# Three-layer transformer in one launch: single scoring in the third mixer's window attention, and a wider in-flight limit in the stick-breaking layer

## The chip, the cores and the metric

The kernel runs on one core of a Trainium2 chip. The metric is the device time of one launch in microseconds (us), the median of several runs. Engines are named as in the profile: PE is the matrix engine (PEld its weight loads), DVE the vector engine, ACT the scalar engine, POOL the GpSimd engine, SP the engine that issues the weight loads by DMA.

## The reference, cut to what matters

256 tokens of width 1024 pass three layers, each a mixer and a convolutional feed-forward net (FFN), in fp32. The mixers differ:

- Layer 1, stick-breaking attention, 16 heads of width 64. For the causal part of a head's scores z, `a = exp(log_sigmoid(z) + suffix)`, where `suffix` is the sum of `log_sigmoid(-z)` over the later keys; the output is `a @ v`.
- Layer 2, a sparse attention that picks keys with an indexer (8 index heads of width 64, 16 attention heads of width 128).
- Layer 3, half window attention, half a gated recurrence. The window attention has 8 query heads of width 64 over 2 key heads:

```python
scores = where(mask, q @ k.T * 64**-0.5, -inf)          # causal window of 128
m = maximum(scores.max(-1), sink)
e = exp(scores - m)
p = e / (e.sum(-1) + exp(sink - m))
out = p @ v
```

Its output is normalised and joined with the recurrence's; one output product follows. The scale, shift and gate vectors of each layer come from a long matrix-vector product of the condition with `ada_w`.

## The kernel before, in words

All activations are kept transposed (features on partitions, 256 tokens along the row). Weights stream from HBM in blocks of 1 MB (`raw`), and each half block of 128x1024 is split into a high and a low part, `wh` on ACT (L409) and `wl` on DVE (L421); a product is three matmuls (`three`, L302: high x high, high x low, low x high). One `unit` (L579) makes 256 output columns from two half blocks, 48 matmuls. Each half block is one *turn*: `next` (L435) counts a tick and releases what earlier turns put off (`after`, `turnover`), the matmuls follow, and `post` (L459) emits a share of the condition's matrix-vector product (`ada_op`, L544: one 512 KB load issued on POOL, L525, and one pass over it on DVE, L532, three buffers) and then takes `rate` steps of the background work (`advance`, L476).

The background work of a mixer is a generator, `heads_in_flight` (L485). A step of it may multiply a pair of finished heads with the values (`product`), do the second stage of one head (`middle`, called `suffix` in layer 1, `flip` in layer 3), and start new heads (`scores`). `a` counts heads started, `c` heads past the second stage; new ones start while `a - c` is below a limit (L491). Its argument `pair` says how many heads one call of `scores` takes, `lag` how many turns lie between a head's scores and its second stage. When a mixer's projections end, `output` (L1103) first lets no head start until none is open (`hold`), then sets `out`, takes the four PSUM banks tagged `acc` for the output product and runs its eight `down` steps between the remaining heads, which now score into the two banks tagged `mm`.

A head keeps its bank from its scores to the end of its second stage. There are four `acc` banks (L310).

- In layer 1 (`stick`, L1003), `scores` (L1034) takes two heads: their four fp32 matmuls have 64 rows each, one head on the upper half of the array's rows, one on the lower, in alternation and `chained` (L316: kept in that order). The softplus of a head runs on ACT (L1051 to L1053, two buffers `e`), DVE (L1057, into `s`, four buffers) and POOL (mask, L1031); `suffix` (L1061) sums with three matmuls, an exponential on ACT and a mask on POOL; `product` (L1070) follows.
- In layer 3 (`mixed`, L1343), `scores` (L1451) also takes two heads in a chain of four 64-row matmuls, adds the mask to each with one more matmul (L1461), and `softmax` (L1464) puts off maximum and exponential by one turn, the division by two. `flip` (L1491) transposes a head's three 128x128 blocks into its own bank and copies them out on ACT (L1129, which frees the bank), `product` (L1494) multiplies a pair with the values, and `window` (L1508) normalises. Then comes `recurrence` (L1598), in the same list of background work: one first step (`acc` banks, L1600), then eight levels, each with decays (`level_decay`, L1554) and scores (`level_scores`, L1577). The first output step needs `window`, the next three need the recurrence.
- In layer 2, `scores` has always taken one head a call.

The Tile framework sets the final order: what the program emits earlier has the higher priority, and a planner with its own model of times lays out each engine's queue, which the engine then works through in order. So a step of the generator sets a priority and not a time.

Of the kernel before, what the change touches and what calls it, by code (L numbers as in the profile page):

```python
# [270 lines left out]
class Prog:  # L271
# [213 lines left out]
    def heads_in_flight(self, n, st, ready, scores, middle, product, lag=2, pair=1):  # L485

        st.update(hold=False, out=False, done=0, open=0, ready=0, split=0)
        a = c = 0
        ticks = {}
        while st["done"] < n:  # L490
            can = a < n and not st["hold"] and ready(a) and a - c < (3 - pair if st["out"] else 4 - pair)  # L491
            did = False
            if st["done"] + 1 < c and (st["done"] % 4 or not st["split"]):
                product(st["done"])
                st["done"] += 2
                did = True
            if c < a and (a - c >= 2 or not can) and self.tick - ticks[c] >= lag and c - st["done"] < WP:
                middle(c)
                c += 1
                did = True  # L500
            if can:
                scores(a)
                for a in range(a, a + pair):
                    ticks[a] = self.tick
                a += 1
                did = True
            st["open"] = a - c
            yield did
# [834 lines left out]
    def mixed(self):  # L1343
        nc, I = self.nc, self.I
        blocks = ((0, slice(0, 128)), (1, slice(128, 384)))
        with ExitStack() as outer:
# [4 lines left out]
            band_r = sk.tile([128, 384], F32R, name="band")  # L1351
# [39 lines left out]
            ka = sk.tile([128, T], F32, name="ka")  # L1391
            va = sk.tile([128, 2, 128], F32, name="va")
            st, part = {}, []
            sp = pool("hgx", 2)
            qa = sp.tile([128, 4, T], F32, name="ro")
# [35 lines left out]
            for half in range(2):  # L1431
                h, l = self.next()
# [10 lines left out]
            def keys():  # L1443
                nc.scalar.activation(ka, bkv[:, 0:T], AF.Identity, bias=self.v("bka"))
                nc.vector.tensor_tensor(va, bkv[:, 256:512].rearrange("p (t c) -> p t c", t=2),
                                        rows[:, None, 512:640].to_broadcast([128, 2, 128]), op=ALU.add)
                self.bg.extend([self.heads_in_flight(8, st, lambda h: True, scores, flip, product, 2, 2), window()])

            Z, E, P, PO = {}, {}, {}, {}

            def scores(h0):  # L1451
                for h in (h0, h0 + 1):
                    Z[h] = self.bank("acc")
                chain = []
                for t, j in ((1, 1), (1, 0), (0, 1), (0, 0)):
                    r = slice(j * 64, j * 64 + 64)
                    chain.append(self.mmul(Z[h0 + j][:, t * 128:128 + t * 256], qa[r, h0 // 2, t * 128:t * 128 + 128],
                                           ka[r, 0:128 + t * 128], start=t == 1))
                self.chained(chain)
                for h in (h0, h0 + 1):  # L1460
                    self.mmul(Z[h][:, 0:384], self.ident_r, band_r, stop=True)  # L1461
                    softmax(h)

            def softmax(h):  # L1464
                i, kv = divmod(h, 2)
                z = Z[h]
                sink = self.v("sink", i + 4 * kv, 1)
                m = sp.tile([128, 4, 2], F32, name="wm", bufs=3)
                e = E[h] = sp.tile([128, 384], F32, name="we", bufs=3)

                def soft():
                    for t, c in blocks:
                        nc.vector.tensor_reduce(m[:, 0, t:t + 1], z[:, c], axis=AX.X, op=ALU.max)
                    nc.vector.tensor_scalar(m[:, 1], m[:, 0], sink, -1.0, op0=ALU.max, op1=ALU.mult)
                    for t, c in blocks:
                        self.act(e[:, c], z[:, c], AF.Exp, bias=m[:, 1, t:t + 1],
                                             accum_out=m[:, 2, t:t + 1])
                    self.act(m[:, 3], m[:, 1], AF.Exp, bias=sink)

                def divide():  # L1480
                    nc.vector.tensor_tensor(m[:, 2], m[:, 2], m[:, 3], op=ALU.add)
                    nc.vector.reciprocal(m[:, 2], m[:, 2])
                    for t, c in blocks:
                        if DM:
                            nc.scalar.activation(e[:, c], e[:, c], AF.Copy, scale=m[:, 2, t:t + 1])
                        else:
                            nc.vector.tensor_scalar(e[:, c], e[:, c], m[:, 2, t:t + 1], None, op0=ALU.mult)
                self.after(1, soft)
                self.after(2, divide)
# [18 lines left out]
            def window():  # L1508
                o = ao
                cs = self.bank("po")  # L1510
                sq, other = [self.squares(o[:, i:i + 2]) for i in (0, 2)]
                nc.vector.tensor_tensor(sq, sq, other, op=ALU.add)
                yield True
                for j in range(2):
                    self.sums(cs[:, 0:2], sq[:, j], j == 0, j == 1)
                rr = self.rsqrt(cs[:, 0:2], 2, 512)
                if FW:
                    self.fence = self.newton[1]
                yield True
                self.spread(cs[:, 256:512], rr, start=False)  # L1520
                for i in range(4):
                    last = nc.vector.scalar_tensor_tensor(o[:, i], o[:, i], self.v("ag", i, 1), cs[:, 256:512], op0=ALU.mult,
                                                   op1=ALU.mult)
                if FW > 1:
                    self.fence = last.ins
                if WS:
                    for i in range(0, 4, WS):
                        self.split_act(oh[:, i:i + WS], ol[:, i:i + WS], o[:, i:i + WS])
                else:
                    self.split_act(oh[:, 0:4], ol[:, 0:4], o)  # L1530
                part.append(0)

            self.after(1, keys)

            def turn():
# [199 lines left out]
```

## Time and profile before

| | us |
|---|---|
| runs of the kernel before | 1038.05, 1036.2, 1028.79; median 1036.2 |
| the profiled execution | 1033.1, of it 1031.4 in its span |
| PE busy | 998.2 (97% of the span) |
| DVE, ACT, POOL busy | 833.5, 636.4, 98.9 |

The span begins with layer 1's norm; its heads lie at 65 to 150 us, its FFN at 160 to 350, layer 2 at 350 to 480 and its FFN to 675, layer 3's mixer at 675 to 830, its FFN to the end. A busy PE is not a PE at its peak: the three-matmul stream places 8.41 matmuls in a us (841 in the 100 us from 200 to 300), and where fewer are placed the difference is waiting or slower forms.

### The profile page before, as it was taken

To read this page: it belongs to the slowest core of one execution; us is meant where nothing else is said; L and a number is where in the kernel's file an instruction comes from. 1 tells how busy PE (TensorE), PEld (TensorE's weight loads), DVE (VectorE), ACT (ScalarE), POOL (GpSimd) and SP (SyncE) were. 2 spreads that over 40 slices of the span, in tenths; PEclk is the share of its full clock that TensorE was granted. 3 is DMA by queue.
4 is the path that set the end of the run, shared out by engine and by line. 5 is a ranking of instruction groups with operands and counts; after the bars stand their busy time and mean duration, and the time that the engine had idled before them with its cause. 6 is when DMAs were issued, how large, how long until landed. Compare 5 with 4: busy or idle time off the path is not lost.

```text
span 1031.4 us, 19958 instructions
## 1 busy us (share of the span) xinstructions
PE 998.2 (97%) x7984; PEld 964.1 (93%) x7984; DVE 833.5 (81%) x1550; ACT 636.4 (62%) x1095; POOL 98.9 (10%) x180
## 2 busy tenths in 40 slices
PE   7999989999999999998999999999999999999996
PEld 5998878999999989988999999999899999999996
DVE  6956768999999889987998889897994588566664
ACT  6575647855555684886965555588854378445543
POOL 0015530011111010110000101100120000000000
PEclk9999989999999999999999999999986999999998
DMA  9969764578888476642767777745880336566531
GB/s 362 405 239 336 243 241 159 209 276 300 290 295 289 142 275 216 241 169 83 268 225 268 283 268 284 277 150 210 306 312 21 124 127 226 200 210 220 211 137 42
DMA packets 45647, 235.66 MB, mean 228 GB/s; under 512 B 5361, under 2 KB 5889, under 8 KB 27889
## 3 DMA queue, kind: packets, MB, share of 16 engines
q1 hardware_dynamic: 25922, 164.21, 44.1%
q0 software_dynamic: 19344, 69.78, 19.3%
q8 instruction: 62, 1.02, 0.4%
q10 hardware_dynamic: 288, 0.39, 0.1%
q14 instruction: 31, 0.25, 0.1%
HBM read 233.29 MB, written 1.07 MB: 227 GB/s over the span
## 4 chain that ended last, share of the span: by engine, by line
PE 81%; issue 8%; DVE 5%; DMA 3%; ACT 2%; POOL 1%; DVEq 0%; SPq 0%; POOLq 0%; ACTq 0%
PE acc L300 32%; PE mm L300 29%; PE po L300 10%; PE small L300 10%; DMA adaw<-ada 2%; DVE x L691 1%; DVE xl L687 1%; POOL adaw L525 1%; DVE wl L421 1%; DVE adaw L532 1%; ACT wh L409 0%; DMA x<-xT 0%; DVE sq L714 0%; PE acc L1126 0%; ACT e L330 0%
## 5 line engine op out<-in xcount | busy, mean ns | idle before, releaser
L409 ACT ACTIVATE wh<-raw 128x1024 fp32r<-128x1024 f32 x290 | 304.7, 1057 | 224.8 <-PE acc L300 87.1
L421 DVE TENSOR_TENSOR wl<-raw,wh 128x1024 fp32r<-128x1024 f32 x290 | 353.0, 1223 | 96.1 <-PE acc L300 27.8
L300 PE MATMUL mm<-xh,wh 128*128 128x256 f32 (+1 forms) x872 | 244.5, 285 | 2.1 <-ACT wh L409 2.1
L300 PE MATMUL mm<-xl,wh 128*128 128x256 f32 (+1 forms) x872 | 245.4, 283 | 0.7 <-DVE xl L687 0.7
L300 PE MATMUL mm<-xh,wl 128*128 128x256 f32 (+1 forms) x872 | 244.3, 282 | 0.0
L532 DVE SCALAR_TENSOR_TENSOR adaw<-adaw,cond 128x1024 f32<-128x1024 f32 x144 | 175.2, 1221 | 10.7 <-DMA adaw<-ada 10.4
L300 PEld LDWEIGHTS mm<-xh,wh 128*128 128x128 f32 x872 | 163.5, 189 | 4.9 <-ACT wh L409 2.7
L300 PEld LDWEIGHTS mm<-xl,wh 128*128 128x128 f32 x872 | 164.6, 189 | 2.3 <-DVE xl L687 1.1
L300 PEld LDWEIGHTS mm<-xh,wl 128*128 128x128 f32 x872 | 164.0, 188 | 0.5 <-issue 0.3
L300 PE MATMUL acc<-gh,wl 128*128 128x256 f32 x528 | 149.0, 283 | 0.0
L300 PE MATMUL acc<-gh,wh 128*128 128x256 f32 x528 | 148.1, 282 | 0.0
L300 PE MATMUL acc<-gl,wh 128*128 128x256 f32 x528 | 147.9, 281 | 0.0
L525 POOL DMA_DIRECT2D adaw<-ada x125 | 66.6, 533 | 738.6 <-DVE adaw L532 624.9
L300 PEld LDWEIGHTS acc<-gl,wh 128*128 128x128 f32 x528 | 100.3, 190 | 0.2 <-DVE gl L337 0.2
L300 PEld LDWEIGHTS acc<-gh,wh 128*128 128x128 f32 x528 | 98.8, 188 | 0.0
L300 PEld LDWEIGHTS acc<-gh,wl 128*128 128x128 f32 x528 | 98.8, 187 | 0.0
L300 PE MATMUL small<-xh,wh 128*128 128x256 f32 x240 | 67.6, 282 | 0.0
L300 PE MATMUL small<-xh,wl 128*128 128x256 f32 x240 | 67.5, 281 | 0.0
L300 PE MATMUL small<-xl,wh 128*128 128x256 f32 x240 | 67.3, 281 | 0.0
L300 PE MATMUL acc<-oh,wh 128*128 128x256 f32 x192 | 53.1, 297 | 2.0 <-ACT oh L336 1.5
L300 PE MATMUL acc<-xh,wl 128*128 128x258 f32 (+1 forms) x192 | 52.4, 284 | 2.1 <-DVE wl L421 2.0
L300 PE MATMUL acc<-ol,wh 128*128 128x256 f32 x192 | 53.7, 286 | 0.4 <-DVE ol L337 0.4
(310 smaller groups left out, 2073.9 us busy)
## 6 DMA issues: line engine op xcount, KB each, us to landing
raw<-ffn SPq DMA_DIRECT2D x99, 1024.0 KB, 5.0
adaw<-ada POOLq DMA_DIRECT2D x125, 512.0 KB, 5.2
raw<-dsa SPq DMA_DIRECT2D x15, 1024.0 KB, 6.4
raw<-hg SPq DMA_DIRECT2D x15, 1024.0 KB, 5.9
adaw<-ada SPq DMA_DIRECT2D x19, 512.0 KB, 10.2
raw<-sb SPq DMA_DIRECT2D x16, 512.0 KB, 10.2
raw<-sb SPq DMA_DIRECT2D x8, 1024.0 KB, 8.5
bias<-scr POOLq DMA_DIRECT2D x8, 256.0 KB, 8.3
```

What stands on the lines that cost most here:

```text
L300: return self.nc.tensor.matmul(o, a, b, start=start, stop=stop, skip_group_check=True).ins
L409: inst = nc.scalar.activation(h[:, :k * n], self.raws[b][:, c0:c0 + k * n], AF.Copy).ins
L421: inst = nc.vector.tensor_tensor(l[:, :k * n], self.raws[b][:, c0:c0 + k * n], h[:, :k * n], op=ALU.subtract).ins
L525: self.nc.gpsimd.dma_start(raw, self.I[f"ada{L}"][b])
L532: return self.nc.vector.scalar_tensor_tensor(w, w, 1.0, self.cond[n // 24], op0=ALU.mult, op1=ALU.mult, accum_out=self.M[n // 12][:, n % 1 ...
L687: return lambda: nc.vector.scalar_tensor_tensor(self.xl[:, m, 0:T], self.x[:, m], a, self.xh[:, m, 0:T], op0=ALU.mult, op1=ALU.subtract)
L691: self.lastx = nc.vector.scalar_tensor_tensor(self.x[:, m], o, self.gate(L, h, m), self.x[:, m], op0=ALU.mult, op1=ALU.add).ins
```

## The change

The limit of heads in flight becomes 3 before `out`, for every caller: for a caller with pairs (layer 1) it was 2, so that a pair now starts while up to two heads are open; for callers with single heads it was 3 already. During `out` the limit stays `3 - pair`. Layer 3 now calls `heads_in_flight` with its defaults (lag 2, pair 1), and its `scores` takes one head, without a chain. The chain in `product` stays.

```diff
@@ heads_in_flight
-            can = a < n and not st["hold"] and ready(a) and a - c < (3 - pair if st["out"] else 4 - pair)
+            can = a < n and not st["hold"] and ready(a) and a - c < ((3 - pair) if st["out"] else 3)
@@ mixed
-                self.bg.extend([self.heads_in_flight(8, st, lambda h: True, scores, flip, product, 2, 2), window()])
+                self.bg.extend([self.heads_in_flight(8, st, lambda h: True, scores, flip, product), window()])
 
-            def scores(h0):
-                for h in (h0, h0 + 1):
-                    Z[h] = self.bank("acc")
-                chain = []
-                for t, j in ((1, 1), (1, 0), (0, 1), (0, 0)):
-                    r = slice(j * 64, j * 64 + 64)
-                    chain.append(self.mmul(Z[h0 + j][:, t * 128:128 + t * 256], qa[r, h0 // 2, t * 128:t * 128 + 128],
-                                           ka[r, 0:128 + t * 128], start=t == 1))
-                self.chained(chain)
-                for h in (h0, h0 + 1):
-                    self.mmul(Z[h][:, 0:384], self.ident_r, band_r, stop=True)
-                    softmax(h)
-
-            def softmax(h):
+            def scores(h):
                 i, kv = divmod(h, 2)
-                z = Z[h]
+                r = slice(kv * 64, kv * 64 + 64)
+                z = Z[h] = self.bank("acc")
+                self.mmul(z[:, 0:128], qa[r, i, 0:128], ka[r, 0:128], start=True)
+                self.mmul(z[:, 128:384], qa[r, i, 128:256], ka[r, :])
+                self.mmul(z[:, 0:384], self.ident_r, band_r, stop=True)
                 sink = self.v("sink", i + 4 * kv, 1)
...
```

## Rows read from the trace of the kernel before

**Rows 1.** The page, part 1: busy time of each engine, share of the span, instructions.
```profile
PE 998.2 (97%) x7984; PEld 964.1 (93%) x7984; DVE 833.5 (81%) x1550; ACT 636.4 (62%) x1095; POOL 98.9 (10%) x180
```

**Rows 2.** Busy time by stage; columns: stretch, length, engines (x instructions), granted clock, DMA.
```profile
65.00:98.00 33.00, 33.00 (x255) 29.84 (x255) 21.57 (x30) 22.61 (x40) 16.15 (x25) 1.00 0.76 276
98.00:108.40 10.40, 8.39 (x63) 6.31 (x62) 6.76 (x12) 8.27 (x20) 3.24 (x7) 1.00 0.81 283
108.40:150.00 41.60, 36.68 (x261) 31.94 (x261) 31.03 (x58) 18.88 (x38) 21.40 (x35) 0.92 0.73 244
200.00:300.00 100.00, 100.00 (x841) 100.00 (x841) 91.64 (x143) 54.84 (x72) 10.61 (x20) 1.00 0.80 282
704.00:759.00 55.00, 53.76 (x440) 50.37 (x439) 48.98 (x105) 44.37 (x102) 9.03 (x17) 1.00 0.77 285
759.00:806.00 47.00, 44.44 (x257) 42.82 (x255) 27.38 (x63) 20.00 (x51) 2.65 (x5) 0.67 0.27 90
```

**Rows 3.** Timeline of PE at a visit to one, four and two heads: start, length, what.
```profile
387.33 0.28 PE L300 MATMUL mm<-xh,wl 128*128 128x256 f32 x1
387.54 0.92 PE L300 MATMUL acc<-ki,qi 64*128 64x128 f32 x4
388.39 0.39 PE L300 MATMUL mm<-xh,wh 128*128 128x256 f32 x1
...
378.64 1.68 PE L300 MATMUL acc<-ki,qi 64*128 64x128 f32 x16
380.26 0.38 PE L300 MATMUL mm<-xh,wh 128*128 128x256 f32 x1
...
707.11 0.92 PE L300 MATMUL acc<-ka,ro 64*128 64x256 f32 x8
707.96 0.62 PE L300 MATMUL acc<-band,ident_r 128*128 128x384 f32 x2
708.42 0.28 PE L300 MATMUL mm<-xh,wh 128*128 128x256 f32 x1
```

**Rows 4.** Timeline of PE, then ACT: the last pair of heads of layer 3.
```profile
732.67 0.70 PE L300 MATMUL acc<-ka,ro 64*128 64x256 f32 x2 [0.76 <-ACT pT L1129]
...
737.73 0.92 PE L300 MATMUL acc<-ka,ro 64*128 64x256 f32 x6
...
734.42 0.49 ACT L1129 ACTIVATE pT<-acc 128x384 f32<-128x384 f32 x1 [0.64 <-PE acc L1126]
```

**Rows 5.** Instructions of the tile qk: duration min/median/max, first and last start.
```profile
L300 PE MATMUL acc<-qk x40: 269/374/481, 65.1 to 103.3; 64*128 64x256 f32 x20, 64*128 64x128 f32 x20
...
L300 PE MATMUL mm<-qk x24: 269/374/480, 97.8 to 136.6; 64*128 64x256 f32 x12, 64*128 64x128 f32 x12
```

**Rows 6.** Timeline of PE in layer 1: scores, and suffix sums of two pairs.
```profile
65.14 1.58 PE L300 MATMUL acc<-qk 64*128 64x256 f32 x16
...
105.86 0.70 PE L300 MATMUL acc<-s,nu 128*128 128x256 f32 x2 [1.50 <-POOL s L1031]
...
112.60 0.60 PE L300 MATMUL acc<-s,nu 128*128 128x256 f32 x2
...
122.67 0.70 PE L300 MATMUL mm<-qk 64*128 64x256 f32 x2
...
135.93 0.92 PE L300 MATMUL mm<-qk 64*128 64x256 f32 x8
```

**Rows 7.** Timeline of all engines at the end of layer 1's heads.
```profile
141.15 1.23 DVE L532 SCALAR_TENSOR_TENSOR adaw<-adaw,cond 128x1024 f32<-128x1024 f32 x1 [0.29 <-DMA adaw<-ada]
...
142.30 1.02 DVE L1057 SCALAR_TENSOR_TENSOR s<-mm,e 128x384 f32<-128x384 f32 x2
...
148.59 0.87 PE L300 MATMUL po<-a,V 128*64 128x256 f32 x8 [1.12 <-POOL a L1031]
...
149.94 0.74 PE L300 MATMUL acc<-oh,wh 128*128 128x256 f32 x4 [0.48 <-ACT oh L336]
```

**Rows 8.** The chain that ended last, 98 to 151 us: start, length, what.
```profile
136.60 4.52 DMA adaw<-ada
```

## The prediction

> **What bounds the kernel now.** I read the page first, then the busy time by stage, then the timelines of the two stretches that the change touches, and last the chain that ends each of them. PE is busy 97% of the span [rows 1], so the question is at what rate it works. In the FFN it places 841 matmuls in 100 us, 8.41 a us, at a granted clock of 1.00 [rows 2]; nothing is to be had there. Two stretches fall behind. In layer 1 from 108.4 to 150 us, where the last heads run between the output's weights, there are 261 in 41.6 us, 6.3 a us; at the FFN's rate they would take 31.0 us. In layer 3 the projections go on until 759 us at 8.0 a us, and then 47 us follow with 257 matmuls, 5.5 a us, at a mean granted clock of 0.67: the tail of the recurrence. The reader should see there that DVE and ACT are only 58% and 43% busy: engines wait for one another.
>
> What ends layer 1's stretch is not the heads alone. The chain [rows 8] passes through a load of `adaw` of 4.52 us; the DVE pass over it runs at 141.15, and heads 14 and 15 have their softplus step at 142.30, right behind it in the same queue; their product follows at 148.59 and the last output step at 149.94 [rows 7].
>
> **Part 1, the limit in layer 1.** I stepped through the generator by hand, two steps a turn, with its own rules. Before, pairs are emitted in turns 0, 1, 3, 4 and 6, so ten heads start before `out` and six after. The trace has it so: 40 matmuls of `qk` into `acc` and 24 into `mm`, four records a head [rows 5]. With the new limit pairs come in turns 0, 0, 2, 3, 4 and 6: twelve heads before `out`, four after, and the last product comes in turn 14 instead of 15. No instruction is added or removed; only priorities move.
>
> What is it worth? Heads in `mm` go one pair at a time: the scores of heads 12 and 13 begin at 122.67, those of 14 and 15 at 135.93 [rows 6], so a pair costs 13.3 us there, and one such pair goes. But the pass at 141.15 needs its load, whichever head is in flight, and the pass ends at 142.3; if the heads were done by then, the last output step could start at 142.3 instead of 149.94, 7.6 us earlier [rows 7]. That is the upper end unless the loads come earlier too. The other side: `hold` now has two more heads to finish before all four `acc` banks go to the output. Two successive pairs there lie 112.60 - 105.86 = 6.7 us apart [rows 6], so the output's weights could start 6.7 us later, with nothing but heads to fill PE, in a stretch where it now places 63 matmuls in 10.4 us [rows 2]. Below both ends stands the fact that at 65.14 sixteen matmuls run together, four heads in the kernel of before [rows 6]: the planner had already filled all four banks, and a higher priority can't make a fifth. So the ends are 7.6 us won and 6.7 us lost. I take 4 us won, about half of the upper end: later pairs do move up a turn, masks and softplus steps with them, and the load that caps it has a row of its own.
>
> **Part 2, single scoring in layer 3.** The pair's chain lays two heads of 64 rows beside each other. Eight records of two heads take 707.96 - 707.11 = 0.85 us, and a single head of the same shape in layer 2, alone, takes 388.39 - 387.54 = 0.85 us [rows 3]. But of the four pairs only two ran whole. The last one (and likewise the third) was broken: its first matmul, 0.70 us, ran at 732.67 as soon as one bank was free, the other six records at 737.73 [rows 4]. So the scores take now 2 x 0.85 + 2 x (0.70 + 0.85) = 4.8 us. After the change: all eight alone, 8 x 0.85 = 6.8 us; but four single heads of layer 2, which no chain orders, took 380.26 - 378.64 = 1.62 us, 0.40 a head [rows 3], because the planner laid them side by side. By the order of emission heads 2 and 3, and 6 and 7, still come in the same turn, 4 x 0.40 + 4 x 0.85 = 5.0 us. I take 5.9, between the two: 1.1 us lost (ends: 1.6 won with all eight in company, 2.0 lost). The mask matmuls: two take 0.46 us behind a pair [rows 3]; one alone costs at least half and at most all of that, so eight cost between nothing and 1.8 us more; I take 0.4, nearer the half, since the form is the same. Entering such a visit costs 387.54 - 387.33 = 0.21 us instead of the 0.12 between two matmuls of the stream [rows 3]; eight visits instead of six add 0.2 us. Together 1.7 us lost on PE, in a stretch that has no slack for it (8.0 of 8.41 a us).
>
> The Trainium skill (TensorEngine Tiling, Theoretical Speedup) gives up to twice the speed for a contraction of 64 rows or less, which speaks against taking pairs apart. This trace agrees where a pair runs whole, 0.85 us for two heads as for one. By the page alone the loss would be 8 x 0.85 - 4 x 0.85 = 3.4 us instead of 1.1, and the whole forecast 2.3 us later.
>
> **Part 3, what the single heads let go earlier.** Now head 6 and head 7 wait for two banks at once. The second was freed at 734.42 + 0.49 = 734.9, the six records came at 737.73, and the first bank lay with a lone matmul from 732.67 [rows 4]; so their softmax could begin 2.8 to 5.1 us earlier. In the generator the last product comes in turn 8 instead of 9, and the recurrence, next in the list, a turn sooner. A turn is 55 us / 14 half blocks = 3.9 us here [rows 2]. What moves out of the tail is work that PE still has to do among the weights: 3.9 us of the tail is 21 matmuls, 2.5 us at 8.41 a us, so 1.4 us are won. Ends: nothing (if the planner had the recurrence's first step where its banks come free anyway) and 5.1 us. I take 1.4. DVE, ACT and POOL have the same instructions as before; in layer 2 the limit is 3 and 2 as before.
>
> **The sum.** 4.0 won in layer 1, 1.7 lost and 1.4 won in layer 3: 3.7 us less. The profiled execution took 1033.1 us (1031.4 in its span), which becomes 1029.4. The median of the runs is 1036.2, 3.1 us above the profiled one, and on that footing the forecast is 1032.5 us.
>
> **Rivals.**
> - *Nothing moves.* The four banks were full before, so priorities change little; layer 1 gives 0, layer 3 0.3 lost, up to 2. For it: 65.14 in [rows 6]. Against it: the broken pairs and the waits for two banks [rows 4] are real. 1036 to 1038 us.
> - *A whole pair goes.* With two heads fewer in `mm`, fewer masks stand on POOL before the loads that it issues, the loads come earlier and the 7.6 us no longer cap the gain. Layer 1 wins 7.6 to 13.3, layer 3 5.1 - 1.7 = 3.4: 1025.2 down to 1019.5 us. For it: the pair's 13.3 us [rows 6]. Against it: the load in the chain [rows 8].
> - *The drain costs more than it saves* (the slower side). Its place is the end of layer 1's projections, its price the 6.7 us by which four banks come free later, while the last pass of `adaw` and what hangs on it shift with the output's turns; with eight lone heads, dear masks and two more visits in layer 3 (2.0 + 1.8 + 0.2 = 4.0), 1036.2 + 10.7 = 1046.9 us. It decides from the point at which the suffix sums of heads 10 and 11 lie more than 7.6 us behind the 112.60 of heads 8 and 9 now: then the pair that is saved later no longer pays.
>
> **How the numbers follow.** Forecast 0.43, nothing moves 0.25, a whole pair 0.18, the drain 0.14. A measurement of this kernel tells about 1% from no change, here 10.4 us: faster means below 1025.8, slower above 1046.6. Faster has most of the second rival (0.15) and a little of the forecast's own spread (0.05): 0.20. Slower has a bit over half of the drain's chance, since milder drains end under the line: 0.09. The rest, 0.71, is the same. The range runs from 1022, inside the second rival, to 1043, inside the drain's; that leaves out about a tenth on each side. The likeliest case alone is 1028 to 1036.
>
> **What would show it.** Right: 48 records of `qk` into `acc` and 16 into `mm`; the last output step of layer 1 at 142 to 148 instead of 149.94; `ka` matmuls in visits of four records, 5.0 to 6.8 us in all; last projection of layer 3 a little after 759, and the tail behind it 1 to 5 us shorter than 47. Wrong: layer 1's output starting after 115 and ending after 150; a pass of `adaw` that still ends the chain with the heads long done (then the cap was all); or a time that moves in an FFN or in layer 2, where nothing was changed.

## The result, and the profile after

The kernel after takes 1024.71 us (median of 20 runs, 1018.71 to 1033.44) against 1031.8 us (20 runs, 1028.45 to 1038.05) for the kernel before: ratio 0.9927, 95% interval 0.9909 to 0.9945. That is 0.73%, 7.5 us (the medians themselves lie 7.1 us apart), about twice the forecast 3.7 us and inside the range. Medians, ratios and mean clocks below are of fast runs; seven of the later runs, 1036.52 us to 5383.13 us long, were in a slow state. The profiled execution took 1025.47 us, 1023.7 of it in its span.

The stages that the change touches, as busy time by stage (columns as in [rows 2]):

```profile
108.40:150.00 41.60, 39.29 (x301) 34.93 (x302) 34.63 (x66) 22.00 (x46) 20.43 (x34) 1.00 0.75 259
704.00:756.00 52.00, 51.97 (x402) 46.74 (x401) 44.92 (x98) 41.77 (x96) 8.46 (x16) 1.00 0.73 262
756.00:796.60 40.60, 37.62 (x274) 35.80 (x272) 29.09 (x68) 22.20 (x55) 3.17 (x6) 0.87 0.38 132
```

Against [rows 2] the end of layer 1's heads places 301 matmuls instead of 261 in the same 41.6 us, at a granted clock of 1.00 instead of 0.92. Layer 3's projections end at 756.0, and the tail behind them is 40.6 us instead of 47.0, at 0.87 instead of 0.67. PE is busy 97% of the span, as before; the reader sees again that this share tells nothing of the rate.

The instructions of the tile `qk`, the counterpart of [rows 5]:

```profile
L300 PE MATMUL acc<-qk x48: 269/374/481, 65.3 to 110.1; 64*128 64x256 f32 x24, 64*128 64x128 f32 x24
...
L300 PE MATMUL mm<-qk x16: 269/374/480, 101.3 to 132.9; 64*128 64x256 f32 x8, 64*128 64x128 f32 x8
```

Twelve heads score into `acc` and four into `mm`; the last one starts at 132.9 instead of 136.6. Then the output's matmuls of layer 1 (tile `oh`), first of the kernel before, then of the kernel after; the last two times of a row are the first and the last start:

```profile
L300 PE MATMUL acc<-oh,wh x64: 277/282/387, 108.4 to 154.4; 128*128 128x256 f32 x64
```

```profile
L300 PE MATMUL acc<-oh,wh x64: 278/281/388, 112.2 to 149.3; 128*128 128x256 f32 x64
```

The output begins 3.8 us later and ends 5.1 us earlier. The chain that ended last there, of the kernel after (start, length, what), the counterpart of [rows 7, 8]:

```profile
139.94 2.30 DVE adaw L532 x4
...
142.27 0.25 DVE mod L558
...
142.53 0.52 POOL adaw L525
...
143.09 0.43 POOL a L1031
...
143.56 0.90 PE po L300 x8
...
144.92 0.99 PE acc L300 x6
```

The last output step runs at 144.92 instead of 149.94. The chain still passes two `adaw` passes, and behind them the mask of the last head on POOL, which stands in POOL's queue after the issue of a load. Whether these passes set the end is not to be read from a chain alone; an experiment below asks it. PE's own timeline of the kernel after already raises a doubt, for PE waited only 0.23 us for that mask:

```profile
143.56 0.87 PE L300 MATMUL po<-a,V 128*64 128x256 f32 x8 [0.23 <-POOL a L1031]
```

Layer 3's single heads on PE, the counterpart of [rows 3]:

```profile
704.56 0.92 PE L300 MATMUL acc<-ka,ro 64*128 64x128 f32 x4
705.41 0.44 PE L300 MATMUL acc<-band,ident_r 128*128 128x384 f32 x1
705.78 0.92 PE L300 MATMUL acc<-ka,ro 64*128 64x128 f32 x4
...
730.88 0.44 PE L300 MATMUL acc<-band,ident_r 128*128 128x384 f32 x1
731.16 0.28 PE L300 MATMUL mm<-wh,xl 128*128 128x256 f32 x1
...
732.99 0.44 PE L300 MATMUL acc<-band,ident_r 128*128 128x384 f32 x1
733.45 0.87 PE L300 MATMUL po<-pT,va 128*64 128x256 f32 x8
734.25 0.92 PE L300 MATMUL acc<-ka,ro 64*128 64x128 f32 x4
```

All eight heads run in visits of four records, each by itself, 705.41 - 704.56 = 0.85 us, also where two follow each other at once: the mask of the first (705.41) stands between heads 0 and 1.

Last, two stretches that can be laid beside each other in every profile below: layer 1 from 60 us to its first residual step (DVE `x` at L691), and layer 3's mixer from the last residual step of the FFN ahead of it to its own first one. The kernel before, then after:

```profile
60.00:151.00 91.00, 84.07 (x626) 74.09 (x625) 60.43 (x100) 53.34 (x102) 40.78 (x67) 0.96 0.74 259
674.90:824.40 149.50, 144.98 (x1086) 139.56 (x1086) 114.20 (x244) 94.95 (x207) 13.49 (x26) 0.90 0.54 194
```

```profile
60.00:145.90 85.90, 81.01 (x627) 72.21 (x626) 61.22 (x99) 53.31 (x102) 41.76 (x67) 1.00 0.76 269
672.30:814.80 142.50, 138.80 (x1086) 131.33 (x1086) 113.25 (x244) 95.90 (x207) 13.48 (x26) 0.96 0.57 203
```

Layer 1 is 5.1 us shorter, layer 3's mixer 7.0 us, with the same number of matmuls. Together that is more than the runs show, for the stages without a change are longer by 4.1 us. In both stretches the clock differs too. A mean of 0.90 over 149.5 us means that PE had 1.2 GHz instead of 2.4 for 2 x 0.10 x 149.5 = 30 us.

### The profile page after: what moved, and what is told of

Read it like the earlier page. It is cut to its first block, busy times and chain, and to the rows that moved or that the text cites. A ratio compares the mean times of both kernels' runs of the same rounds, so it can differ in the third digit from the quotient of the medians.

```text
span 1023.7 us, 19966 instructions
## 1 busy us (share of the span) xinstructions
PE 992.4 (97%) x7984; PEld 957.5 (94%) x7984; DVE 833.2 (81%) x1550; ACT 637.0 (62%) x1095; POOL 99.8 (10%) x180
## 4 chain that ended last, share of the span: by engine, by line
PE 80%; issue 9%; DVE 5%; ACT 2%; DMA 2%; POOL 2%; DVEq 0%; SPq 0%; POOLq 0%; ACTq 0%
PE acc L300 32%; PE mm L300 28%; PE po L300 10%; PE small L300 10%; DVE x L691 1%; DVE xl L687 1%; DMA adaw<-ada 1%; POOL adaw L525 1%; DVE adaw L532 1%; DVE wl L421 1%; DVE sq L714 1%; DMA x<-xT 0%; POOL s L1031 0%; PE acc L1126 0%; ACT wh L409 0%
## 5 line engine op out<-in xcount | busy, mean ns | idle before, releaser
L300 PE MATMUL acc<-xl,wh 128*128 128x258 f32 (+1 forms) x192 | 54.8, 289 | 0.0
L300 PE MATMUL acc<-xh,wh 128*128 128x258 f32 (+1 forms) x192 | 54.7, 294 | 0.0
```

The lines of the kernel that those rows point to most:

```text
L300: return self.nc.tensor.matmul(o, a, b, start=start, stop=stop, skip_group_check=True).ins
```

## The experiments

All were timed in five rounds beside the kernel before, whose medians lay between 1031.2 and 1032.29. A gain in us below is the ratio's distance from 1, taken of these; the figures in brackets are 95% intervals. The theory after the result: layer 1's limit gives its 4 us, and layer 3 gives more than forecast because heads reach the tail earlier. Its rival: layer 3's gain is the clock's. At the end a table holds what the runs and profiles have in common.

**The kernel before, once more.**

> The kernel before, once more, for the granted clock of each of its runs: the one profile of before shows 0.979, the runs of the kernel after 0.981 to 0.996, and among those a run with less clock is longer by about 8 us for each hundredth. If the gain is mostly clock (theory A), before has a mean clock near 0.980; if it is mostly work taken out of the waits (theory B), its clock is near that of after, 0.990. The time itself is that of before, ratio 1.000.

1030.77 us, ratio 0.9995 (0.9972 to 1.0017). The mean clock of its runs is 0.985, half way between the 0.980 of theory A and the 0.990 of theory B. Its profile, the same two stretches:

```profile
60.00:151.20 91.20, 84.23 (x632) 74.40 (x631) 61.35 (x99) 53.22 (x102) 41.34 (x67) 0.96 0.74 258
675.60:819.90 144.30, 135.96 (x1086) 129.94 (x1086) 113.66 (x245) 94.47 (x207) 13.49 (x26) 0.96 0.57 200
```

This is the most useful row of the study. The unchanged program has a mixer of 144.3 us here and of 149.5 us in the first profile, with 1086 matmuls in each, and the clock is 0.96 and 0.90. So 5.2 of the 7.0 us that the two first profiles show in layer 3 lie within what one kernel does from one execution to the next; layer 1's 151.2 repeats to 0.2 us. The tail shows the same. From 756 to 830 us, first in the first profile of before, then in this one, then in the kernel after:

```profile
756.00:830.00 74.00, 71.03 (x480) 69.21 (x478) 49.35 (x109) 33.24 (x78) 4.24 (x8) 0.79 0.34 117
756.00:830.00 74.00, 66.00 (x511) 63.36 (x509) 55.12 (x120) 36.18 (x82) 4.76 (x9) 0.93 0.37 126
756.00:830.00 74.00, 69.01 (x524) 66.78 (x523) 54.80 (x122) 37.37 (x84) 4.23 (x8) 0.91 0.34 116
```

In clock and matmuls the unchanged program's second execution is nearer to the kernel after than to its own first one.

**Layer 1's limit alone** (kernel before, limit 3 for its 16 heads, layer 3 as it was):

```diff
-            can = a < n and not st["hold"] and ready(a) and a - c < (3 - pair if st["out"] else 4 - pair)
+            can = a < n and not st["hold"] and ready(a) and a - c < (3 - pair if st["out"] else (3 if n == 16 else 4 - pair))
```

> The new limit in layer 1 alone, layer 3 as before. If the two parts add up as the marks of the two profiles have it (first residual of layer 1 at 145.9 instead of 151.0, layer 3's mixer 7.0 us shorter, 4 us given back in other stages), 5.1 us or less are won, ratio 0.995 to 0.997, with the last output step of layer 1 at about 145. If layer 1's change only moves the clock's drop, nothing is won, 1.000. If all of the gain is layer 1's, 0.993.

1026.97 us, ratio 0.9958 (0.9928 to 0.9988): 4.3 us.

```profile
60.00:146.30 86.30, 81.40 (x630) 72.63 (x629) 61.43 (x100) 53.30 (x102) 42.23 (x67) 1.00 0.75 267
673.60:822.90 149.30, 142.20 (x1086) 136.50 (x1086) 113.48 (x245) 94.75 (x207) 13.47 (x26) 0.92 0.54 194
```

Layer 1 ends at 146.3 as in the kernel after, and layer 3 is as long as in the first profile of before; but the profiled execution took 1033.0 us, 6 us above this kernel's median, so its 149.3 us stand for one of the longer executions. By its runs the limit is worth what the forecast said, within an interval of 1.2 to 7.4 us. That it is only part of the 7.5 is likely but not shown by these two kernels alone, whose intervals overlap (0.9928 to 0.9988, and 0.9909 to 0.9945).

**Single heads alone** (kernel after, with the old expression of the limit, so that layer 1 is as before):

```diff
-            can = a < n and not st["hold"] and ready(a) and a - c < ((3 - pair) if st["out"] else 3)
+            can = a < n and not st["hold"] and ready(a) and a - c < (3 - pair if st["out"] else 4 - pair)
```

> Single scoring in layer 3 alone, layer 1 as before. If the parts add, 3 to 7 us are won, ratio 0.993 to 0.997, with the last projection of layer 3 near 89.8 us after the mixer before it ended and the tail about 41 us long instead of 48. The forecast's own terms had 0.3 us lost here: ratio 1.000.

1030.64 us, ratio 0.998 (0.9955 to 1.0005): 2.1 us, not told apart from nothing. With the 4.3 us of the limit it makes 6.4, so for single heads the two parts add up to the 7.5 within the intervals. Its layer 1 ends at 149.1 at a clock of 1.00, its mixer:

```profile
673.10:819.80 146.70, 141.61 (x1086) 133.56 (x1086) 113.16 (x245) 96.23 (x207) 13.41 (x26) 0.94 0.56 197
```

**The limit for all, heads of layer 3 still in pairs** (kernel before, limit expression of after):

```diff
-            can = a < n and not st["hold"] and ready(a) and a - c < (3 - pair if st["out"] else 4 - pair)
+            can = a < n and not st["hold"] and ready(a) and a - c < ((3 - pair) if st["out"] else 3)
```

> The new limit for every caller, but layer 3 still scores in chained pairs, now with four heads in flight. If the single scoring itself matters (no pair waits for two banks), layer 3 stays near its old length and the ratio is that of the run with the limit in layer 1 alone. If what matters there is only that heads are emitted earlier, layer 3 gains as much as with single heads, or more, as the pairs save up to 2 us of PE: ratio 0.990 to 0.993.

1025.25 us, ratio 0.9934 (0.9906 to 0.9962): as fast as the kernel after. Taking the pairs apart is not needed for the gain. A pair that may start while two heads are open makes four, where single heads at limit 3 and pairs at the old limit 2 reach three.

```profile
674.10:815.90 141.80, 133.21 (x1076) 127.52 (x1076) 113.94 (x244) 95.55 (x207) 13.46 (x26) 0.98 0.56 204
```

**Filling the tail** (24 matmuls, whose results nobody reads, into a spare bank behind each of four rounds of `level_decay`; once in the kernel before, once in after):

```diff
+                def fill(n):
+                    for _ in range(n):
+                        i = self.mmul(spare[:, 0:256], gh[:, 0, 0], lev[:, 0:2].rearrange("p a b -> p (a b)"),
+                                      start=True, stop=True)
+                        self.behind(i, st["last"])
+                        st["last"] = i
...
+                    fill(24)
```

> The kernel before, with 24 idle matmuls (128x256 into a bank that nobody reads, 96 in all, 11.4 us of PE at 8.41 a us) behind each of the four rounds of decays in layer 3's recurrence, so that PE does not rest there. Theory A (the time of layer 3 hangs on how long its tail runs at half clock): the half clock in the tail, 30.7 us and 10.2 us in the two profiles of before, goes to almost nothing, the mean granted clock of the runs rises from 0.983 to 0.992 or more, and by 7 us for each hundredth up to 6 us are won less what the idle matmuls delay: ratio 0.994 to 1.000. Theory B (the waits set the tail, the clock only follows): the clock rises, but nothing is won and the idle matmuls cost some us: ratio 1.002 to 1.010.

> The same idle matmuls in the kernel after. Its tail ran at half clock for 10.2 us in its profile, and its runs have a mean clock of 0.990. Theory A: little is left to win, ratio to before 0.990 to 0.995, so between 3 us faster and 2 us slower than the kernel after. Theory B: slower than the kernel after by what the idle matmuls delay, 3 us or more: ratio 0.996 and up.

In the kernel before: 1030.99 us, ratio 0.9982 (0.9962 to 1.0002). In after: 1028.16 us, 0.9933 (0.9903 to 0.9963), not told apart from after's 0.9927 (its median is 3.4 us higher). Both ratios are those of theory A. The tail and the mixer, of the kernel before with the filling:

```profile
756.00:797.00 41.00, 40.43 (x345) 39.45 (x343) 28.10 (x65) 20.00 (x50) 2.65 (x5) 1.00 0.33 112
```

```profile
671.90:816.40 144.50, 141.97 (x1182) 137.15 (x1182) 113.45 (x245) 94.88 (x207) 13.42 (x26) 1.00 0.57 200
```

and the mixer of after with it:

```profile
669.10:817.90 148.80, 145.36 (x1182) 137.92 (x1181) 113.55 (x244) 95.55 (x207) 13.39 (x26) 1.00 0.55 194
```

96 more matmuls raise the tail's clock to 1.00, and the mean over the runs of the kernel before from 0.982 to 0.991: the clock follows what PE does. They also cost about what it gives back, so filling wins nothing that can be measured here. With the tail at full clock in both profiles, after still leads before by 0.9982 - 0.9933 = 0.5%, 5.1 us, of which layer 1's limit is 4.3. This speaks for the rival, but the intervals are 0.2% and 0.3% wide to either side and leave room for all of layer 3's 3.2 us; after's mixer is even the longer one here, in a single profile.

**Single heads, two in flight** (kernel after, limit 2 for the eight heads of layer 3):

```diff
-            can = a < n and not st["hold"] and ready(a) and a - c < ((3 - pair) if st["out"] else 3)
+            can = a < n and not st["hold"] and ready(a) and a - c < ((3 - pair) if st["out"] else (2 if n == 8 else 3))
```

> The kernel after with a limit of 2 in layer 3 alone: heads are scored singly, but at most two may be open when one starts. If the gain in layer 3 comes from more heads in flight (earlier emission), it goes, and the time is that of the limit in layer 1 alone or worse by the lost pairing: ratio 0.996 to 0.999. If it comes from single scoring, it stays: 0.992 to 0.994.

1031.56 us, ratio 0.9987 (0.9965 to 1.0008). Layer 1 ends at 146.4, and yet hardly anything of the gain is left.

```profile
673.80:820.60 146.80, 138.36 (x1086) 130.03 (x1086) 114.11 (x245) 95.52 (x207) 13.48 (x26) 0.95 0.55 197
```

The third head in flight is worth 0.6%, 6.2 us, and this is clear of the intervals. Beside layer 1's limit alone (0.9958), singles with two in flight lose 0.3%, 3.0 us, which isn't: that single scoring has a price is read from PE's records above and not shown by the time. This kernel also has at most two heads open where the pairs had three.

**Fewer loads in layer 1** (kernel after, six of the 24 `adaw` loads and passes left out):

```diff
-        if L > 2:
+        if L > 2 or (i % 4 == 3 and 16 <= i < 40):
...
-        inst = self.ada_one(self.ada_i, k)
+        if k == 3 and self.ada_i < 10:
+            inst = self.nc.vector.memset(self.M[L][:, i, 3:4], 0.0).ins
+        else:
+            inst = self.ada_one(self.ada_i, k)
```

> The kernel after without every fourth load and pass of the condition's product in layer 1 (six of 24; those columns of the scale, shift and gate vectors are set to zero before the bias is added). If the chain of loads and passes caps the end of layer 1, as the forecast's upper end had it, six passes at 1.23 us and their loads move the first residual of layer 1 from 145.9 us to 140 or earlier, and with the 15 us shorter DVE queue the ratio is 0.984 to 0.988. If heads, masks and banks set the end, layer 1 ends within 1.5 us of 145.9 and the ratio stays 0.990 to 0.993.

1025.1 us (7 runs), ratio 0.9917 (0.9885 to 0.995), after's own time. Layer 1's first residual step is at 145.6, in after 145.9. The chain at the end of layer 1 now:

```profile
132.57 7.03 PE acc L300 x57
139.60 0.88 PE mm L300 x6
140.48 0.72 PE acc L300 x6
141.19 0.89 PE mm L300 x6
...
142.71 0.42 POOL a L1034
...
144.53 1.00 PE acc L300 x6
```

No load and no pass is left in it. From 132.57 to 142.1 it is PE alone, working through the output's weights with the last heads' sums between them, and the last output step comes 0.4 us earlier. A chain names the releaser that came last; behind it PE's queue stood almost as late.

**Single heads, four in flight** (kernel after, limit 4 for layer 3's heads):

```diff
-            can = a < n and not st["hold"] and ready(a) and a - c < ((3 - pair) if st["out"] else 3)
+            can = a < n and not st["hold"] and ready(a) and a - c < ((3 - pair) if st["out"] else (4 if n == 8 else 3))
```

> The kernel after, with up to four single heads in flight in layer 3 (there are four acc banks) instead of three. If heads in flight carry layer 3's gain and the third was not yet enough: 1 to 3 us below the kernel after's 1024.7, so 1022 to 1024. If three were already all that can be used, since the second stages and not the starts set the pace: the kernel after's time within its noise, 1024 to 1026, with the tail behind the last projection again near 40 us. If early heads in the fourth bank hold up the recurrence's first step, which takes its banks from the same four: 1026 to 1030.

1024.48 us, ratio 0.9935 (0.991 to 0.9961): nothing beside after's 0.9927, as forecast for the case that three are all that can be used. But the tail isn't near 40 us, as that case had it: the last projection starts at 763.8, 59.6 us behind the first scores (before 51.0), and the first output step behind the tail at 795.0. Work did move out of the tail and in among the weights, and the time stayed.

```profile
672.00:813.20 141.20, 136.69 (x1086) 129.76 (x1086) 112.93 (x245) 95.32 (x207) 13.47 (x26) 0.98 0.58 205
```

**The limit for layer 3's pairs alone** (kernel before, limit 3 where `n == 8`):

```diff
-            can = a < n and not st["hold"] and ready(a) and a - c < (3 - pair if st["out"] else 4 - pair)
+            can = a < n and not st["hold"] and ready(a) and a - c < ((3 - pair) if st["out"] else (3 if n == 8 else 4 - pair))
```

> The kernel before with one edit: in layer 3 a chained pair may start while up to two heads are open (limit 3); layer 1 keeps its limit 2. If the parts add, it is worth what separates the limit in both layers from the limit in layer 1 alone (ratios 0.9934 and 0.9958): 2.5 us, so about 1029.5 to 1030, with layer 1's first residual back at 151 us and layer 3's mixer some 149 us long. If layer 3's gain is only the clock's, which an unchanged kernel also shows from one execution to the next: 1032 (no change), and a mean granted clock over the runs like the kernel before's 0.983.

1032.97 us, ratio 1.0027 (1.0004 to 1.005). I expected 2.5 us less; it is 2.8 us more. For pairs the parts do not add, though only just clear of the intervals: what the wider limit gives layer 3's pairs behind the new layer 1 (0.9934 against 0.9958) it does not give behind the old one. Here too the tail is shorter (39.5 us from the last projection's start at 766.39 to the first output step behind it at 805.85, in before 48.1), and the projections longer. Layer 1 ends at 149.4 here; the mixer:

```profile
677.20:824.10 146.90, 137.86 (x1086) 131.63 (x1086) 113.50 (x245) 95.83 (x207) 13.40 (x26) 0.95 0.56 197
```

**Fewer loads in layer 3** (the last eight of its 24 left out, in before and in after):

```diff
-        if L > 2:
+        if L > 2 or i >= 136:
...
-        inst = self.ada_one(self.ada_i, k)
+        if self.ada_i >= 34:
+            inst = self.nc.vector.memset(self.M[L][:, i, k:k + 1], 0.0).ins
+        else:
+            inst = self.ada_one(self.ada_i, k)
```

> The kernel before without the last eight of layer 3's 24 adaw loads and passes (eight small memsets of M stand in their place, so the last two groups of the condition's product are left out). In before's chain a load of 6.36 us and the pass at 758.01 lie ahead of the X steps with which the recurrence's tail begins. If loads and passes set the tail's start: 2 to 4 us less than the kernel before, 1028 to 1030. If the tail is set by its own chain from PE to DVE and back, as layer 1's end was set by PE's queue: less than 1 us, 1031 to 1033.

> The same omission in the kernel after, whose chain passes a load of 8.14 us and the pass at 767.33. If loads set the tail and the change only moved the heads out of their way, the distance between this kernel and e10_before_fewer shrinks from 7.5 to the 4.3 us of layer 1's limit. If layer 3's gain has nothing to do with the loads, the distance stays 6 to 8 us, and this kernel takes 1023.5 to 1025.5.

Before without them: 1032.57 us, ratio 1.0017 (0.9988 to 1.0047). After without them: 1026.93 us, 0.9944 (0.9916 to 0.9973), above the expected 1023.5 to 1025.5. Neither is faster than with them, and the ratios stay 0.73% apart, 7.5 us. The loads do not set the tail either, though both chains pass through one. The mixer of before without them:

```profile
677.30:820.80 143.50, 134.51 (x1086) 128.49 (x1086) 113.35 (x244) 94.36 (x207) 11.83 (x23) 0.98 0.54 191
```

**All together.** Mixer's length and clock are those of the rows above (after without the eight loads has 143.3 us at 0.98); the last column is the mean granted clock over the runs of the kernel. Layer 1's and the mixer's columns are of one execution each.

| kernel | layer 1's first residual, us | mixer of layer 3, us, clock | ratio | clock, mean of runs |
|---|---|---|---|---|
| before | 151.0 | 149.5, 0.90 | | 0.983 |
| before, again | 151.2 | 144.3, 0.96 | 0.9995 | 0.985 |
| before, fewer loads | 151.0 | 143.5, 0.98 | 1.0017 | 0.982 |
| limit in layer 1 | 146.3 | 149.3, 0.92 | 0.9958 | 0.986 |
| limit for layer 3's pairs | 149.4 | 146.9, 0.95 | 1.0027 | 0.985 |
| singles alone | 149.1 | 146.7, 0.94 | 0.998 | 0.985 |
| singles, two in flight | 146.4 | 146.8, 0.95 | 0.9987 | 0.986 |
| limit for all, pairs | 146.8 | 141.8, 0.98 | 0.9934 | 0.989 |
| singles, four in flight | 144.6 | 141.2, 0.98 | 0.9935 | 0.989 |
| after | 145.9 | 142.5, 0.96 | 0.9927 | 0.990 |
| after, fewer loads | 146.2 | 143.3, 0.98 | 0.9944 | 0.988 |

Two things are to be seen. The first column falls into two groups by layer 1's limit alone: 148.0 to 151.2 in six profiles with the old one (with the filled kernel's 148.0), 144.3 to 146.8 in eight with the new one (144.3 in after filled, 145.6 with fewer loads in layer 1); the means, 150.0 and 145.8, are 4.2 us apart. The mixer's length, on the other hand, goes with its clock more than with the kernel: at 0.98 it is 141.2 to 143.5 us, at 0.94 to 0.95 it is 146.7 to 146.9 us, whatever was changed.

## Why the prediction was right, and where not

The direction and the range were right, and so was the split of heads. The likeliest case's own range, 1028 to 1036, was missed from below. Two things moved it: the median of 1036.2 on which the forecast stood is 1031.8 over 20 runs, and the gain was 7.5 us instead of 3.7. The forecast gain is half of the measured one, and of its parts only part 1 has the right size, by luck.

- **Part 1, 4.0 won: right in size.** By itself the limit gives 4.3 us. The split of 48 and 16 records came as stepped by hand, and the output began 3.8 us later, within the 6.7 put down for it. *The step that failed is the cap.* The pass at 142.3 was held to be the limit of what could be won, since its load needs its time; with six loads fewer the last output step moves by 0.4 us. What stands behind it is PE's own queue: 57 of the output's matmuls without a wait from 132.57 us on and the last heads' sums after them, and in the kernel after a wait of only 0.23 us before the last product. Half of an upper end that wasn't one gave the right number, and only the number.
- **The clock in layer 1** had a row, 0.92 in [rows 2], and no term. In three of six profiles with the old limit there is a stretch at 1.2 GHz before the first residual step (151.0, 151.2, 151.0), in three none (149.1, 149.4, 148.0); with the new limit there is none in eight. Beside those three alone the limit gains 148.8 - 145.8 = 3.0 us, so by an estimate about 1.2 of the 4.2 is the clock's.
- **Part 2, 1.7 lost on PE: too small.** The choice between company and alone failed: each head's mask follows its own scores, so that even heads 0 and 1, one right behind the other, had a mask between them, and heads 6 and 7 a mask and a product (732.99 to 734.25). All eight ran alone, 8 x 0.85 = 6.8 us, the upper end (2.0 lost instead of 1.1). A mask alone takes 0.28 to 0.46 us (731.16 - 730.88, 733.45 - 732.99), 2.6 us for the eight against 8 x 0.23 = 1.8 in pairs: 0.8 lost instead of 0.4. With the forecast's 0.2 for visits that is 3.0 us. The 3.0 us that singles with two in flight lose beside layer 1's limit alone agree with it, but that figure isn't clear of its intervals, and that kernel also holds fewer heads open. The Trainium skill (TensorEngine Tiling (Array Packing), Theoretical Speedup) gives up to twice the speed where a dimension is 64 or less. The trace agrees: a head alone takes 0.85 us, as long as a whole pair. The loss was 2.0 us instead of the 3.4 that the page alone would give, because two of the four pairs had been broken.
- **Part 3, 1.4 won: mis-sized, and one term was missing.** The tail is 6.4 us shorter between the first two profiles, above the 1 to 5 that were to show it right; but from the last projection's start to the first output step behind the tail it is 40.6 us in after, 48.1 in before and 42.8 in before once more, so that most of it isn't shown to be the change's. Beside layer 1's limit alone, layer 3's part is worth 0.9958 - 0.9927 = 0.3%, 3.2 us, where the forecast had 0.3 lost; the two intervals overlap. Among single heads the limit carries it, by two, three and four in flight (0.9987, 0.9927, 0.9935). The count alone can't be all, since the pairs at the old limit reach three open heads as well.
- **Part 3's mechanism.** *The step that failed is the overlap.* The forecast had a turn's work moved out of the tail. In the kernel after it wasn't: the last projection is at 756.05, 51.5 us behind the first scores, in before 758.09 and 51.0, and the tail holds 274 matmuls, not fewer than the 257. In the three kernels with four open heads it was, the tail being 31.2 to 39.5 us long, and of these two are no faster than after and one (1.0027) no faster than before.
- **The clock in the tail.** What differs between the first two profiles is the tail's clock, 0.67 to 0.87, that is 31 to 11 us at 1.2 GHz, and the forecast had no term for a clock that depends on how densely PE is fed. Before's repeat has only 10 us at 1.2 GHz in its tail (0.88), without any change.
- **The sum.** Some 4.3 of the 7.5 us are layer 1's limit, some 3.2 layer 3's. Seen the other way, over all runs the clock rises from 0.983 to 0.990. Within one kernel the runs lie on a slope of 6 to 9 us for 0.01 of mean clock, so at about 7.5 us some 5 of the 7.5 us go along with the clock (an estimate; that the clock makes them is not shown). The 2 to 3 that are left are no more than layer 1's 3.0. What stays open is how far layer 3's change makes that clock: the filled kernels and the heads-in-flight series speak for density, and the pairs alone (1.0027) say that it doesn't follow from the limit in layer 3 by itself.
- **Rivals.** *Nothing moves* fell with the interval. *A whole pair goes* would have named the time, 1025, but not the cause: the loads didn't come earlier (last pass at 141.01 against 141.15), and loads are not what ends the stretch. *The drain* had its point of decision, sums of heads 10 and 11 more than 7.6 us behind 112.60; they began at 118.84, 6.2 behind, so the pair that was saved still paid.
- **Stages without a change** moved by up to 1.6 us each, 4.1 us in all and all to the slower side: layer 2's mixer took 129.7 us instead of 128.1, with a short stretch at 1.2 GHz at its start that the profile of before didn't have.

## What to carry to other kernels

Where PE waits in short pieces, read the granted clock of the stretch and give it a term of its own: a change that brings work closer together can be paid twice, once in waits and once in clock, and the second part shifts from run to run. Profile the unchanged kernel a second time before a difference of a few us between two profiles is explained. An operation on the chain is a suspect and not yet the cause: leave it out and see what stands behind it.

## What was not expected of the hardware

- One program's layer 3 mixer took 149.5 and 144.3 us in two executions, with granted clocks of 0.90 and 0.96: 5.2 us more went with about 18 us more at 1.2 GHz (2 x 0.10 x 149.5 - 2 x 0.04 x 144.3), 0.3 us each.
- 96 matmuls whose results nobody reads, 24 behind each of four rounds, lifted the tail's clock to 1.00 (345 matmuls in 41 us, before 257 in 47 us, at 0.67) and left the time where it was, 0.9982 (0.9962 to 1.0002).
- Eight loads of 512 KB and their DVE passes could go from the tail, and six from layer 1's heads, with no gain that can be measured, though the chain of waits ran through a load or its pass in each of these places (8.14 us the longest load).
